# Deeper buffers for gathered rows of u, both mark tiles in one, and a final sum by DMA in place of a product with a constant

## The chip, the core and the metric

The kernel runs on one core of one Trainium2 chip. The metric is the time of one execution on the device, in microseconds; the median of three runs is compared.

## What is computed

Two transformer blocks in float32 over 512 tokens of width 1024. The change touches only the end of the second block, a layer of small experts (the reference calls it PEER). For each token and each of 8 heads it chooses 16 of 16384 experts; each expert is one row of `u` and one row of `v`, both 1024 wide:

```python
    e = i1 * N_KEYS + i2                       # chosen experts, 8 x 16 per token
    gate = jax.nn.softmax(best, axis=-1)
    u = u_exp[e]
    v = v_exp[e]
    act = jax.nn.gelu(jnp.einsum("thkd,td->thk", u, xb))
    return jnp.einsum("thk,thkd->td", (gate * act).astype(xb.dtype), v)
...
    x = x + gt2[:, None, :] * peer_ffn(h2, w_peer_q[l], peer_sub_keys[l], peer_u[l], peer_v[l])
    return rmsnorm_2(x, final_g)
```

## The kernel before

The expert layer is done in two ways side by side. The first `NS` = 128 tokens (four groups, `NG` = 4, of 32 tokens) go the sparse way: the rows of `u` and `v` that they chose are gathered from memory. The other `ND` = 384 tokens go the dense way: every expert is computed on TensorE for all of them and weighted by a table that is zero where an expert was not chosen. Float32 products are made from three products of high and low parts (`mm3`, lines 194 to 196; the parts come from `split`, ScalarE at line 148 and VectorE or GpSimd at line 149).

**Stage of the marks (lines 1569 to 1619, about 1446 to 1970 us).** A loop over 48 units of 8 dense tokens. For each unit `marks` (1575) builds two 128x128 marks per token: `G1` on VectorE (gate where the expert's first index agrees, line 1584) and `P2` on ScalarE (one where the second agrees, 1585 and 1586). Their product on TensorE (1604) is the token's table of weights, which ScalarE stages (1606) and stores to `Wd` (1594). `G1` has three buffers under the tag `whi`, `P2` three under the tag `P2`, which the routing's `eq` (1531) used before. In the same loop two experts per unit are made for all dense tokens (`expert_early`, 1417: load of 512 KB of `u`, 1357, split, 24 products, Gelu), and the generator `sparse_u` (1387) is stepped about three times a unit (1611).

`sparse_u` gathers rows of `u`: 128 steps, one for each of 32 choices and 4 groups. A step gathers 128 rows of 4 KB (32 tokens by four quarters of the choices) on GpSimd's queue (1375), and, `nb - 1` steps later, VectorE multiplies the buffer with the tokens and adds up along each row (1405). It has `nb` = 3 buffers: two halves of a tile under `wraw` and `gu3`. Both the gather and the product are kept behind what was written before them for the same engine (`keep_in_program_order`); other instructions are ordered by a planner ahead of time. The weights of the last 128 tokens come out of `pick` (1478, lines 1488 to 1493); the memory of the routing is freed after the last `pick`, and three more buffers for raw `u` (1352) lie in it.

**Stage of v (lines 1622 to 1778, about 1970 to 2550 us).** 32 blocks of four experts: `prepare` (1642) loads `v`, the table and the activations, multiplies and splits them; `products` (1672) adds into eight accumulators `O`, which take all eight PSUM banks. `sparse_v` (1678) is stepped along (1758): gathers of `v` rows into six buffers, each added with its weight into `fin` (`sacc`, 128 x 4 x 1024) by VectorE (1695, 1697). A token's sum then lies in four quarters, on four partitions 32 apart. At its end `sparse_v` brings them together with a product with a constant 0/1 matrix, `fold` (1701 to 1712), adds the residual and normalizes (1713 to 1718), and stores the first 128 tokens (1719). `bank()` there waits for a PSUM bank, and the first is free when `add(0, O[0])` has emptied it in the last block (1766 to 1777). After the last column come a sum over partitions (1782), the norm and the store of the dense tokens (1786 to 1796).

Of the kernel before, what the change touches and what calls it, by code (L numbers as in the profile page):

```python
# [10 lines left out]
F32 = mybir.dt.float32  # L11
# [3 lines left out]
AF = mybir.ActivationFunctionType  # L15
# [6 lines left out]
D = 1024  # L22
# [47 lines left out]
def tile_body(ctx: ExitStack, tc: tile.TileContext, A, out, taps=None, upto=None):  # L70
# [72 lines left out]
    def bank():  # L143
        return psum.tile([128, 512], F32, name="bank", tag="bank")
# [1242 lines left out]
    def sparse_u():  # L1387

        w2 = [wpool.tile([128, 2, D], F32, name=f"gu{i}", tag="wraw", bufs=2) for i in range(2)]
        free = [w[:, i] for w in w2 for i in range(2)]  # L1390
        hr = [xsp.tile([128, D], F32, name="hr", tag="xs") for g in range(min(NG, XS))] + free[:max(0, NG - XS)]
        bufs = free[max(0, NG - XS):] + [up.tile([128, D], F32, name="gu3")]
        nb = len(bufs)
        for g in range(NG):
            nc.sync.dma_start(hr[g], ap(Hd, 32 * g * D, [[0, 4], [D, 32], [1, D]]))
        steps = [(s, g) for s in range(32) for g in range(NG)]
        for k in range(len(steps) + nb - 1):
            if k < len(steps):
                s, g = steps[k]
                gather(bufs[k % nb], A["u_rows"], g, s)  # L1400
            if k >= nb - 1:
                s, g = steps[k - nb + 1]
                b = bufs[(k + 1) % nb]
                d = sr[:, 2, g, s:s + 1]
                tc.keep_in_program_order(nc.vector.tensor_tensor_reduce(  # L1405
                    out=b, in0=b, in1=hr[g], op0=OP.mult, op1=OP.add, scale=1.0, scalar=0.0, accum_out=d))
            yield
        nc.scalar.activation(sr[:, 3], sr[:, 2], AF.Gelu_apprx_tanh)
        nc.vector.tensor_tensor(sr[:, 3], sr[:, 3], sr[:, 1], op=OP.mult)
        while True:  # L1410
            yield
# [25 lines left out]
    with ExitStack() as ph:  # L1437
# [137 lines left out]
        def marks(n):  # L1575

            t, tok0 = divmod(NS + 8 * n, 128)
            i1, i2, gp = picks[t]
            G1 = wpool.tile([128, 8, 128], F32, name="G1", tag="whi", bufs=3)
            P2 = up.tile([128, 8, 128], F32, name="P2", bufs=3)  # L1580
            for k in range(0, 8, 4):
                for i in range(4):
                    tok = slice(tok0 + k + i, tok0 + k + i + 1)
                    nc.vector.tensor_scalar(G1[:, k + i], IOTA, i1[:, tok], gp[:, tok], op0=OP.is_equal, op1=OP.mult)
                    nc.scalar.activation(P2[:, k + i], IOTA, AF.Square, scale=-1.0, bias=i2[:, tok])
                nc.scalar.activation(P2[:, k:k + 4], P2[:, k:k + 4], AF.Relu, scale=-1.0, bias=1.0)
            return G1, P2

# [8 lines left out]
        for n in range(units):  # L1597
# [10 lines left out]
                stores.extend((n // 4, stage, e) for e in range(0, 128, 32))  # L1608
            if stores:
                store()  # L1610
            while 32 * NG + 6 > fed[0] and fed[0] * (units - 4) < (n + 1) * (32 * NG + 6):
                next(sparse)
                fed[0] += 1
            while (n + 1) * (N_EARLY * BT - routed) // units > early[0] - routed:
# [7 lines left out]
    with ExitStack() as ph:  # L1622
# [55 lines left out]
        def sparse_v():  # L1678
# [7 lines left out]
            for k in range(len(steps) + nb - 1):  # L1686
# [10 lines left out]
                        tc.keep_in_program_order(nc.vector.scalar_tensor_tensor(  # L1697
                            fin[:, g], b, w, fin[:, g], op0=OP.mult, op1=OP.add))
                yield
            x, row, sq = (b[:NS] for b in bufs[:3])  # L1700
            FOLD = bufs[4][:, :NG * NS]
            nc.sync.dma_start(FOLD, A["fold"])
            ssq = small.tile([128, 1], F32, name="fsq", bufs=1)
            nc.sync.dma_start(x, Xd[0:NS, :])
            nc.sync.dma_start(row, ap(Mv, 5 * D, [[0, NS], [1, D]]))
            for f in range(2):
                c = slice(f * 512, (f + 1) * 512)
                o = bank()
                for g in range(NG):
                    nc.tensor.matmul(o[:NS], FOLD[:, g * NS:(g + 1) * NS], fin[:, g, c], start=g == 0, stop=g == NG - 1)  # L1710
                nc.vector.tensor_tensor(row[:, c], o[:NS], row[:, c], op=OP.mult)
                nc.vector.tensor_tensor(x[:, c], x[:, c], row[:, c], op=OP.add)
            yield
            nc.vector.memset(ssq, 1.0)
            nc.scalar.activation(sq, x, AF.Square, accum_out=ssq[:NS])
            nc.sync.dma_start(row, ap(A["final_g"], 0, [[0, NS], [1, D]]))
            r = inv_rms(ssq, D, newton=True)
            nc.vector.scalar_tensor_tensor(x, x, r[:NS], row, op0=OP.mult, op1=OP.mult)
            nc.sync.dma_start(out[0:NS, :], x)
            yield  # L1720

# [27 lines left out]
        for n, b in enumerate(order[:-1]):  # L1749
            nxt = prepare(order[n + 1])  # L1750
            next(nxt, None)
            for group in (range(4), range(4, 8)):
                for i in range(0, BT, 2):
                    products(b, group, i, i + 2)
                    if group[0] or i:
                        next(nxt, None)
                k = 2 * n - 1 + (group[0] > 0)
                while n >= 1 and vfed[0] * 57 < k * (32 * NG + 5):
                    next(gathered, None)
                    vfed[0] += 1  # L1760
            for _ in nxt:
# [66 lines left out]
def lay_out(i):  # L1828
# [1 line left out]
    cols = lambda v: np.ascontiguousarray(v.reshape(-1, 128).T)  # L1830
    a = {}
    a["cst"], a["t5"] = constants()
    a["fold"] = (np.arange(128)[:, None] % 32 + 32 * (np.arange(NG * NS) // NS) == np.arange(NG * NS) % NS).astype(np.float32)
    a["x"] = i["x"][0]
    a["xT"] = a["x"].reshape(4, 128, 8, 128).transpose(0, 3, 2, 1)
    a["mem"] = i["mem"][0]
# [73 lines left out]
```

## Time and profile before

| | |
|---|---|
| median of three runs | 2561.01 us (2559.43 to 2565.94) |
| the profiled execution | 2564.41 us, of which the span is 2562.4 us |
| mean granted TensorE clock | 0.979 of 2.4 GHz |
| TensorE busy | 2452.3 us (96%) |
| VectorE busy | 1753.2 us (68%) |
| ScalarE busy | 1159.9 us (45%) |
| GpSimd busy | 509.8 us (20%) |
| DMA | 545.79 MB, mean 213 GB/s |

The span runs from the first to the last instruction; the profiled execution's own time is 2.0 us longer. Products on TensorE overlap their neighbours, so that a busy TensorE is not one at its peak: the number of products in a stretch says more. PE is TensorE, PEld its loading of weights, DVE VectorE, ACT ScalarE, POOL GpSimd, SP SyncE, whose queue issues most of the DMAs. Where a line is that of a helper (148, 149, 194 to 196, 1375), the name of the tile tells which step it is.

### The profile page before, as it was taken

Reading aid. Unit: us, or ns where it says so; the run is one execution under the profiler, and the core shown is the slowest. Engines: PE = TensorE matmul, PEld = TensorE weight load, DVE = VectorE, ACT = ScalarE, POOL = GpSimd, SP = SyncE. Lnnn points to the kernel's source line nnn. Section 1 sums busy time; section 2 is a strip of 40 time slices with the busy share of each in tenths; the row PEclk is TensorE's granted clock in tenths of the full one; section 3 lists DMA queues with packets and bytes.
Section 4 is the critical chain, followed back from the end, with each engine's and each line's share of the span. In section 5 each row is a group of like instructions: output and inputs, shape, how many; then the busy total and the mean of one; then the engine's idle time right before and its main releaser. Section 6 shows DMA issues by size and latency. Waiting matters only on the chain.

```text
span 2562.4 us, 36881 instructions
## 1 busy us (share of the span) xinstructions
PE 2452.3 (96%) x13565; PEld 2241.0 (87%) x13565; DVE 1753.2 (68%) x4163; ACT 1159.9 (45%) x2339; POOL 509.8 (20%) x389
## 2 busy tenths in 40 slices
PE   8899989999999999999997889999999999999998
PEld 7789878888878888888896789999999899999997
DVE  6467687643374567446889777777773588888884
ACT  7346464323244445224232467767675333333333
POOL 0021000000000000000043344434420144445430
PEclk9899999999999999999998889999999999999999
DMA  8511347742332221334133589999996999999981
GB/s 299 183 63 34 112 154 274 256 171 91 107 131 104 94 87 65 111 132 160 62 101 101 169 323 345 351 345 335 338 332 232 332 340 365 366 370 359 367 302 58
DMA packets 181905, 545.79 MB, mean 213 GB/s; under 512 B 17259, under 2 KB 68003, under 8 KB 170972
## 3 DMA queue, kind: packets, MB, share of 16 engines
q1 hardware_dynamic: 130592, 353.52, 40.0%
q0 software_dynamic: 38944, 139.49, 14.6%
q10 hardware_dynamic: 12188, 50.44, 5.0%
q8 instruction: 106, 1.74, 0.3%
q14 instruction: 75, 0.61, 0.1%
HBM read 480.25 MB, written 67.33 MB: 214 GB/s over the span
## 4 chain that ended last, share of the span: by engine, by line
PE 71%; DVE 10%; issue 9%; POOL 5%; DMA 3%; ACT 2%; POOLq 0%; SPq 0%; DVEq 0%; ACTq 0%
PE bank L196 21%; PE bank L194 21%; PE bank L195 20%; POOL gu L1375 5%; DVE eq L1534 1%; PE bank L1604 1%; DMA gu<-in_u_rows,eS 1%; PE bank L732 1%; PE bank L324 1%; PE bank L735 1%; DVE best L1544 1%; PE bank L323 1%; DMA adaw<-in_w_adaT 1%; PE bank L1164 1%; DVE eq L1538 1%
## 5 line engine op out<-in xcount | busy, mean ns | idle before, releaser
L194 PE MATMUL bank<-hTh,uhl 128*128 128x384 f32 x1024 | 357.7, 349 | 33.8 <-ACT uhl L148 33.8
L196 PE MATMUL bank<-hTh,uhl 128*128 128x384 f32 x1024 | 355.0, 347 | 23.9 <-DVE uhl L149 12.3
L195 PE MATMUL bank<-hTl,uhl 128*128 128x384 f32 x1024 | 352.1, 344 | 0.0
L196 PE MATMUL bank<-wah,vlo 128*128 128x384 f32 x1024 | 347.2, 339 | 0.0
L194 PE MATMUL bank<-wah,vhi 128*128 128x384 f32 x1024 | 346.0, 338 | 0.0
L195 PE MATMUL bank<-wal,vhi 128*128 128x384 f32 x1024 | 344.7, 337 | 0.0
L194 PE MATMUL bank<-hTh,whi 128*128 128x512 f32 (+1 forms) x832 | 318.4, 385 | 1.2 <-ACT hTh L148 1.2
L195 PE MATMUL bank<-hTl,whi 128*128 128x512 f32 (+1 forms) x832 | 315.4, 380 | 1.7 <-DVE hTl L149 1.7
L196 PE MATMUL bank<-hTh,wlo 128*128 128x512 f32 (+1 forms) x832 | 314.9, 379 | 0.2 <-DVE wlo L177 0.2
L1375 POOL DMA_INDIRECT gv<-in_v,eS x107 | 172.3, 1610 | 346.4 <-DVE sacc L1697 182.4
L194 PEld LDWEIGHTS bank<-hTh,uhl 128*128 128x128 f32 x1024 | 198.5, 194 | 36.0 <-ACT uhl L148 36.0
L1375 POOL DMA_INDIRECT gu<-in_u_rows,eS x128 | 178.6, 1395 | 255.1 <-DVE sr L1405 244.4
L196 PEld LDWEIGHTS bank<-hTh,uhl 128*128 128x128 f32 x1024 | 197.9, 193 | 30.9 <-DVE uhl L149 16.2
L148 ACT ACTIVATE wah<-ga 128x384 fp32r<-128x384 f32 x128 | 66.1, 518 | 349.7 <-PE bank L196 343.3
L195 PEld LDWEIGHTS bank<-hTl,uhl 128*128 128x128 f32 x1024 | 198.3, 194 | 0.0
L149 DVE TENSOR_TENSOR wlo<-wraw,whi 128x512 fp32r<-128x512 f32 (+1 forms) x200 | 129.5, 685 | 93.4 <-ACT whi L148 93.1
L196 PEld LDWEIGHTS bank<-wah,vlo 128*128 128x128 f32 x1024 | 192.4, 188 | 0.5 <-issue 0.5
L194 PEld LDWEIGHTS bank<-wah,vhi 128*128 128x128 f32 x1024 | 192.3, 188 | 0.2 <-issue 0.2
L195 PEld LDWEIGHTS bank<-wal,vhi 128*128 128x128 f32 x1024 | 192.1, 188 | 0.2 <-issue 0.2
L195 PEld LDWEIGHTS bank<-hTl,whi 128*128 128x128 f32 x832 | 158.9, 191 | 32.4 <-DVE hTl L149 2.6
L196 PEld LDWEIGHTS bank<-hTh,wlo 128*128 128x128 f32 x832 | 158.4, 190 | 32.4 <-DVE wlo L177 0.6
L194 PEld LDWEIGHTS bank<-hTh,whi 128*128 128x128 f32 x832 | 157.8, 191 | 32.0 <-ACT hTh L148 2.2
(508 smaller groups left out, 5221.0 us busy)
## 6 DMA issues: line engine op xcount, KB each, us to landing
uraw<-in_u SPq DMA_DIRECT2D x128, 512.0 KB, 6.6
vraw<-in_v SPq DMA_DIRECT2D x64, 1024.0 KB, 6.3
adaw<-in_w_adaT SPq DMA_DIRECT2D x48, 512.0 KB, 4.1
Wd<-stage ACTq DMA_DIRECT2D x48, 512.0 KB, 6.5
Wt<-Wd SPq DMA_DIRECT2D x32, 768.0 KB
GAd<-ga ACTq DMA_DIRECT2D x31, 768.0 KB
ga<-GAd SPq DMA_DIRECT2D x31, 768.0 KB, 9.6
wraw<-in_ffn_gu SPq DMA_DIRECT2D x22, 1024.0 KB, 6.6
```

Of the source, the lines that this page charges most:

```text
L148: nc.scalar.activation(hi, src, AF.Copy)
L149: (eng or nc.vector).tensor_tensor(lo, src, hi.bitcast(F32), op=OP.subtract)
L194: nc.tensor.matmul(o, l[0], r[0], start=start, stop=False)
L195: nc.tensor.matmul(o, l[0], r[1], start=False, stop=False)
L196: nc.tensor.matmul(o, l[1], r[0], start=False, stop=stop)
L323: nc.tensor.matmul(o, Q, K[:, g], start=True, stop=False)
L324: nc.tensor.matmul(o, Q, K[:, 2 + g], start=False, stop=stop)
L732: nc.tensor.matmul(o, slot[:, 0, ts(i)], v(i, 0), start=i == 0, stop=i == j)
L735: nc.tensor.matmul(o, slot[:, 1, ts(i)], v(max(0, j - 2) + i, 1), start=i == 0, stop=i == nb - 1)
L1164: nc.tensor.matmul(O[:, 128 * j + 64 * g:128 * j + 64 * g + n], pt[:, ts(i)], va[:, i, 128 * c + 64 * g:128 * c + 64 * g + n], start=i == ...
L1375: tc.keep_in_program_order(nc.gpsimd.indirect_dma_start(out=dst, out_offset=None, in_=src, in_offset=bass.IndirectOffsetOnAxis(ap=eS[:, g, ...
L1534: nc.vector.scalar_tensor_tensor(eq[:, a % 8], cf, float(offs[a]), step[:, :, a:a + 1].to_broadcast([128, 8, 16]), op0=OP.is_ge, op1=OP.mult)
```

## The change

Three things change, and two paces with them. `sparse_u` gets three more buffers, `gu4`, under the tag `P2`, which makes six; the product of a step is written five steps after its gather and no longer two. `G1` and `P2` become two halves of one tile under the tag `whi`, with three buffers, so that the tag `P2` is free for the gathers. The loop of units steps `sparse_u` so that its end still falls inside (137 steps over 45 units in place of 134 over 44).

At the end of `sparse_v` the product with `fold` goes, with its load and the constant. In its place 16 DMAs bring quarter `q` of each group `g` from partitions 32q to 32q+31 of `fin` to the partitions of the group's tokens, in `parts[q]`; three sums on VectorE add up the four parts, and the rest follows on 128x1024 tiles. The pace of `sparse_v` goes from 133 to 139 steps in 57 half blocks.

```diff
         bufs = free[max(0, NG - XS):] + [up.tile([128, D], F32, name="gu3")]
+        bufs += [up.tile([128, D], F32, name="gu4", tag="P2", bufs=3) for _ in range(3)]
         nb = len(bufs)
...
-                b = bufs[(k + 1) % nb]
+                b = bufs[(k - nb + 1) % nb]
...
-            G1 = wpool.tile([128, 8, 128], F32, name="G1", tag="whi", bufs=3)
-            P2 = up.tile([128, 8, 128], F32, name="P2", bufs=3)
+            both = wpool.tile([128, 2, 8, 128], F32, name="marks", tag="whi", bufs=3)
+            G1, P2 = both[:, 0], both[:, 1]
...
-            while 32 * NG + 6 > fed[0] and fed[0] * (units - 4) < (n + 1) * (32 * NG + 6):
+            while 32 * NG + 9 > fed[0] and fed[0] * (units - 3) < (n + 1) * (32 * NG + 9):
...
-            x, row, sq = (b[:NS] for b in bufs[:3])
-            FOLD = bufs[4][:, :NG * NS]
-            nc.sync.dma_start(FOLD, A["fold"])
+            parts, (x, row) = bufs[:4], bufs[4:6]
             ssq = small.tile([128, 1], F32, name="fsq", bufs=1)
             nc.sync.dma_start(x, Xd[0:NS, :])
             nc.sync.dma_start(row, ap(Mv, 5 * D, [[0, NS], [1, D]]))
-            for f in range(2):
-                c = slice(f * 512, (f + 1) * 512)
-                o = bank()
+            for q in range(4):
                 for g in range(NG):
-                    nc.tensor.matmul(o[:NS], FOLD[:, g * NS:(g + 1) * NS], fin[:, g, c], start=g == 0, stop=g == NG - 1)
-                nc.vector.tensor_tensor(row[:, c], o[:NS], row[:, c], op=OP.mult)
-                nc.vector.tensor_tensor(x[:, c], x[:, c], row[:, c], op=OP.add)
+                    nc.sync.dma_start(parts[q][32 * g:32 * g + 32], fin[32 * q:32 * q + 32, g])
+                yield
+                if q % 2:
+                    nc.vector.tensor_tensor(parts[q], parts[q], parts[q - 1], op=OP.add)
+            sq = parts[1]
+            nc.vector.tensor_tensor(sq, sq, parts[3], op=OP.add)
+            nc.vector.tensor_tensor(sq, sq, row, op=OP.mult)
+            nc.vector.tensor_tensor(x, x, sq, op=OP.add)
             yield
...
-                while n >= 1 and vfed[0] * 57 < k * (32 * NG + 5):
+                while n >= 1 and vfed[0] * 57 < k * (32 * NG + 11):
...
-    a["fold"] = (np.arange(128)[:, None] % 32 + 32 * (np.arange(NG * NS) // NS) == np.arange(NG * NS) % NS).astype(np.float32)
```

## Rows read from the trace of the kernel before

**Rows 1.** Stretches of the span, the columns named in the first line

```profile
core 0: us, PE busy (x) PEld busy (x) DVE busy (x) ACT busy (x) POOL busy (x), PEclk, DMA share, GB/s
1460.00:1500.00 40.00, 28.50 (x166) 27.77 (x165) 25.31 (x51) 18.66 (x42) 17.74 (x14) 0.83 0.84 301
1500.00:1910.00 410.00, 405.46 (x2521) 402.50 (x2520) 310.87 (x633) 290.21 (x628) 160.84 (x115) 1.00 0.93 339
...
2050.00:2480.00 430.00, 430.00 (x2454) 430.00 (x2453) 365.22 (x427) 147.07 (x207) 202.07 (x119) 1.00 0.99 358
```

**Rows 2.** Stretches inside the stage of marks: one without holes, one with

```profile
1530.00:1600.00 70.00, 70.00 (x441) 70.00 (x440) 54.45 (x112) 50.21 (x111) 28.62 (x20) 1.00 0.96 347
...
1730.00:1740.00 10.00, 8.42 (x45) 8.42 (x46) 9.45 (x20) 6.00 (x14) 5.23 (x4) 0.83 0.77 259
```

**Rows 3.** All waits in 1500 to 1910: total us, times, longest

```profile
POOL gu L1375 <- DVE sr L1405: 225.5, 88, 4.6
...
DVE gu L1405 <- DMA gu<-in_u_rows,eS: 97.7, 56, 4.5
...
PE bank L196 <- DVE uhl L149: 4.5, 5, 2.0
```

**Rows 4.** DMA issues in 1500 to 1910, median us to landing

```profile
uraw<-in_u SPq DMA_DIRECT2D x79, 512.0 KB, 6.9
...
gu<-in_u_rows,eS POOLq DMA_INDIRECT x115, 8.0
```

**Rows 5.** VectorE's timeline ahead of the hole at 1730: start, duration, [idle <-releaser]

```profile
1725.09 1.23 DVE L1405 CUSTOM_DVE_ANT_0 gu<-gu,hr 128x1024 f32<-128x1024 f32 x1 [1.66 <-DMA gu<-in_u_rows,eS]
...
1729.15 1.23 DVE L1405 CUSTOM_DVE_ANT_0 gu<-gu,hr 128x1024 f32<-128x1024 f32 x1 [2.83 <-DMA gu<-in_u_rows,eS]
...
1730.31 1.22 DVE L149 TENSOR_TENSOR uhl<-uraw,uhl 128x1024 fp32r<-128x1024 f32 x1
```

**Rows 6.** VectorE by line and form, 2050 to 2525: busy, mean ns, idle before

```profile
L1697 DVE SCALAR_TENSOR_TENSOR sacc<-gv,sr,sacc 128x1024 f32<-128x1024 f32 x104 | 130.4, 1277 | 0.0
```

**Rows 7.** VectorE's timeline at the start of the stage

```profile
1470.20 1.23 DVE L1405 CUSTOM_DVE_ANT_0 gu<-gu,hr 128x1024 f32<-128x1024 f32 x1 [9.16 <-DMA gu<-in_u_rows,eS]
...
1471.73 1.23 DVE L1405 CUSTOM_DVE_ANT_0 gu<-gu,hr 128x1024 f32<-128x1024 f32 x1 [0.30 <-DMA gu<-in_u_rows,eS]
...
1472.89 0.28 DVE L1488 CAST eI<-bank 128x128 int32<-128x128 f32 x1
1473.10 1.21 DVE L1405 CUSTOM_DVE_ANT_0 gu<-gu,gu 128x1024 f32<-128x1024 f32 x1
...
1475.41 0.26 DVE L1493 CAST i<-e 128x128 f32<-128x128 int32 x1
```

**Rows 8.** Waits of SP's queue, 1440 to 1500

```profile
SPq L1357 <- DVE i L1493: 14.3, 1, 14.3
```

**Rows 9.** GpSimd's timeline at the start of the stage

```profile
1462.29 0.98 POOL L1375 DMA_INDIRECT gu<-in_u_rows,eS  x1 [0.30 <-issue]
...
1471.71 0.94 POOL L1375 DMA_INDIRECT gu<-in_u_rows,eS  x1 [7.20 <-DVE sr L1405]
```

**Rows 10.** The chain of work that ended last, 2500 to 2563

```profile
2528.25 3.53 PE bank L1710 x8
...
2532.65 3.62 PE bank L1710 x8
```

**Rows 11.** SP's timeline at the end

```profile
2497.78 0.34 SPq L1704 DMA_DIRECT2D gv<-Xd  x1
```

**Rows 12.** VectorE's timeline towards the end

```profile
2496.47 2.47 DVE L1697 SCALAR_TENSOR_TENSOR sacc<-gv,sr,sacc 128x1024 f32<-128x1024 f32 x2
2503.51 0.56 DVE L149 TENSOR_TENSOR wal<-ga,wah 128x384 fp32r<-128x384 f32 x1 [4.56 <-PE bank L195]
...
2531.82 0.69 DVE L1711 TENSOR_TENSOR gv<-bank,gv 128x512 f32<-128x512 f32 x1 [3.79 <-PE bank L1710]
```

**Rows 13.** The marks' lines on ScalarE: ns min/median/max

```profile
L1585 ACT ACTIVATE P<-cst,i x384: 384/390/414, 1434.0 to 1944.9; 128x128 f32<-128x128 f32 x192
```

More of the change, by code (lines that the diff above doesn't have):

```diff
@@ L1705, in sparse_v @@
             nc.sync.dma_start(row, ap(Mv, 5 * D, [[0, NS], [1, D]]))
-            for f in range(2):
-                c = slice(f * 512, (f + 1) * 512)
-                o = bank()
+            for q in range(4):
                 for g in range(NG):
-                    nc.tensor.matmul(o[:NS], FOLD[:, g * NS:(g + 1) * NS], fin[:, g, c], start=g == 0, stop=g == NG - 1)
-                nc.vector.tensor_tensor(row[:, c], o[:NS], row[:, c], op=OP.mult)
-                nc.vector.tensor_tensor(x[:, c], x[:, c], row[:, c], op=OP.add)
+                    nc.sync.dma_start(parts[q][32 * g:32 * g + 32], fin[32 * q:32 * q + 32, g])
[6 more added lines that the diff above has]
+            nc.vector.tensor_tensor(x, x, sq, op=OP.add)
             yield
-            nc.vector.memset(ssq, 1.0)
-            nc.scalar.activation(sq, x, AF.Square, accum_out=ssq[:NS])
+            nc.scalar.activation(sq, x, AF.Square, accum_out=ssq)
             nc.sync.dma_start(row, ap(A["final_g"], 0, [[0, NS], [1, D]]))
             r = inv_rms(ssq, D, newton=True)
-            nc.vector.scalar_tensor_tensor(x, x, r[:NS], row, op0=OP.mult, op1=OP.mult)
+            nc.vector.scalar_tensor_tensor(x, x, r, row, op0=OP.mult, op1=OP.mult)
             nc.sync.dma_start(out[0:NS, :], x)
```

## Prediction

> **What bounds the kernel now.** I read the time by stage first, then the waits inside the stage that holds the gathers, then the chain of waits at the end. In the stage of the marks and the gathers of u, TensorE shows 405 of 410 us busy [rows 1]. A busy share says little here, because neighbouring products overlap, so I count products. An undisturbed stretch makes 441 in 70 us, 6.30 per us [rows 2]; the whole stage made 2521 in 410 us, which at that rate needs 400 us. So about 10 us of it are lost in single holes, the largest of which is a stretch with 45 products where 63 fit, at a clock of 0.83 [rows 2]. (The counts take in products that cross an edge, so this is good to a microsecond or two; adding up the holes alone gives some 8 us.)
>
> What makes the holes: in this stage TensorE waits only for VectorE's low parts of u (line 149), 4.5 us in 5 waits; VectorE waits 97.7 us in 56 waits for gathered rows to land; GpSimd waits 225.5 us in 88 waits for VectorE to have used a buffer [rows 3]. That is a loop: GpSimd may start gather k only when the product of gather k-3 is done, a gather needs 8.0 us to land [rows 4], and VectorE, which works in order, then stands at the next product with the low parts of u queued behind it. In the largest hole one sees it: two products with 1.66 and 2.83 us of idle time ahead of them, and the low part only after both [rows 5]. A unit of 8 tokens has 48 + 16 products in the rows, so 64 / 6.30 = 10.2 us, and carries three gathers: a buffer has one unit in which to be issued, to land and to be used. Some 9.5 us (0.3 to the issue [rows 9], 8.0, 1.2 for the product [rows 5]) stand against 10.2 us. It is on the edge, and small lateness goes through to TensorE.
>
> **Six buffers.** Gather k now waits for product k-6, so there are two units, 20 us, for the same 9.5 us. The two copies of the buffer index are equal for 3 and for 6 buffers (k+1 and k-2, k+1 and k-5 leave the same rest), so that line changes nothing. The pace stays: 137/45 steps a unit against 134/44. The last product comes some three steps, one unit, later, into a stretch where VectorE has time. The nearest row for six buffers is the stage of v: there each gather has six buffers, the DMA engines are busier (0.99 against 0.93) [rows 1], and the sums that use the rows show no idle time ahead of them in 104 instructions [rows 6]. So VectorE's 97.7 us go. What is late next is TensorE itself, for VectorE is busy 311 of 410 us and ScalarE 290 [rows 1]. Bounds: nothing gained, if the holes have another cause that shows only then, to 10 us gained, the whole loss. I take 8 us, the sum of the holes. On the other side, the raw u loads have six buffers and land in 6.9 us [rows 4], and one expert costs TensorE some 5 us (two in a unit), so they could land two or three times as late without harm.
>
> More gathers under way compete for the same DMA engines. The rows show these at 0.93 and 339 GB/s in this stage and at 0.99 and 358 GB/s in the stage of v [rows 1], so 2% more speed in this stage is there to be had, though not 6%. The Trainium skill speaks against the change here (DMA: Bandwidth & Descriptors, Queues, rings and completion order): a DMA engine goes round its queue rows and takes a whole packet from each that has work, so a gather queue that always has work takes its turn each time and the raw loads of u land later. No run here shows that yet; if it went so far that TensorE waited for raw u, the 8 us would drop out of the sum, which is rival (2).
>
> **The start of this stage.** Here 166 products were made in 40 us [rows 1], where 252 would fit: 13.6 us lost, part of it at a lower granted clock (0.83 over the stretch). It is a different chain. VectorE stands at the first product until gather 0 lands at 1470.2, does a second one, and only then the casts of the last pick, 1472.89 to 1475.41 [rows 7]. The next raw loads stand on SP's queue for that last cast, 14.3 us [rows 8], because their new buffers lie in the memory that the routing frees. The change moves the first product one unit later in the program's text, but product 0 is still pinned only behind marks that were made long before, and it needs the same gather, started at the same time. I therefore leave both first products ahead of the casts. The third product (at 1473.10, between the casts) goes behind the next marks, which gives about 1.2 us; three more gathers start at once (gather 3 had waited till 1471.71 [rows 9]), and 3 x 0.52 MB at 358 GB/s is up to 4.4 us of DMA work ahead of the raw loads. Bounds: 13.6 us gained, if the casts come first, to 4.4 us lost; I take 0.
>
> **Both marks in one tile.** No instruction is added or removed. The tile has as many buffers as each had (three), so the distance from unit to unit stays. Cost nothing, if the two halves are tracked apart (below).
>
> **Quarters by DMA, no constant.** The products with the constant are 16 instruction records at the very end. They need a PSUM bank, all eight are taken by the accumulators, so they run when the first accumulator is emptied, in the middle of the last block. There they lie on the chain that ended last with 3.53 and 3.62 us [rows 10], 7.15 us; products follow without a hole to the end. With them gone the chain of the last columns is the same, 7.15 us earlier. The sums now need no PSUM, so they can run one block earlier. Added: 16 DMAs of 128 KB, at 0.34 us of SP each [rows 11] 5.4 us of issuing; three sums, a product and a sum of 128x1024 on VectorE, 5 x 1.22 = 6.1 us by the low part of the same size [rows 5], against four halves of 0.69 us [rows 12], 2.8 us, before. No row shows such a DMA between partitions. The nearest are the loads of 512 KB, 6.9 us [rows 4]; I take 7 us for a quarter. Its cover: the last accumulation ends at 2498.9 [rows 12]; the pace in the stage of v rises by 139/133, so that it ends two half blocks earlier, and a block of 96 products at 175 ns (below) is 16.8 us; VectorE idles 4.56 us at 2503, waiting for TensorE to free buffers [rows 12]. So 6.1 us of sums are hidden. Queued behind the 16 DMAs on SP are the last loads of v, a block ahead of their use. If a sum is put ahead of the last low parts, VectorE stands for a quarter twice, up to 2 x (4 x 0.34 + 7) = 17 us, of which at least 4.6 are covered: a cost between 0 and 12 us. I take 0, since by then VectorE has no accumulations left (133/57 = 2.3 in a half block, 3 us). The faster pace adds under 1% to the traffic of a stage that runs at TensorE's own rate (2454 products in 430 us [rows 1], 175 ns each): nothing.
>
> **The sum.** 8 + 7.15 = 15 us. Against its own time (2564.41, span 2562.4) the profiled execution would come to about 2549; the median of the runs is 3.4 us lower, 2561.0, and from it I forecast 2546.
>
> **Rivals.** (1) The casts come before the first products: then the start's stall goes too. For it: the first products stand a unit later in the text. Against: only what is ready decides there, and that has not moved. 2546 - 13 = 2533. (2) Only the constant's products are saved, because the holes in the u stage stay: with six gathers always under way the raw loads of u land later than TensorE needs them, and the waits change their name. For it: DMA engines at 0.93. Against it: the lead of the raw loads, and [rows 6]. 2561 - 7 = 2554. (3) VectorE stands for quarters ahead of the last splits. 2546 + up to 12 = 2558; for it, that landing takes longer than an order made beforehand allows for. (4) Slower: the marks in one tile are tracked as one, so VectorE's and ScalarE's halves, written in turns, wait for each other. A unit would then hold VectorE for 8 x 0.39 us of ScalarE's marks [rows 13], 3.1 us, on top of the 7.7 us it is busy (311/410 of 10.2): 10.8 against 10.2, 0.6 us in each of 48 units, about 30 us; with the end's 7 us off, 2584. It decides against us as soon as a unit grows by 0.32 us (15/48). Against it: two gathers go into the halves of one tile, and product 0 read one half at 1470.2 while the other landed for 1471.73 [rows 7]; no wait there for the tile as a whole. (5) The change doesn't bite: the gathers are still paced by something else and the sums still land at the very end; 2561.
>
> **How the numbers follow.** Forecast 0.55, (1) 0.15, (2) 0.13, (3) 0.08, (4) and a start that gets worse together 0.06, (5) 0.03. The range, 2532 to 2556, holds the forecast with its bounds, (1), (2) and a part of (3). About 0.3%, 7.7 us, can be told from no change. Faster by more: the forecast nearly always, (1), and a little of (2) and (3), 0.75. Within it: most of (2) and (3), and (5), 0.18. Slower: (4) and a bad start, 0.07.
>
> **What would show it.** Right: VectorE waits for gathers of u only at the start, GpSimd still waits for products, and the stage from 1500 on holds 6.3 products per us throughout; the last block's products run without a break of 7 us, and the store of the first 128 tokens leaves before the last block. Wrong: TensorE waits for raw u; VectorE shows waits for quarters between the last low parts; VectorE's marks wait for ScalarE's; the hole at 1473 is gone or longer.

## The result and the profile after

The changed kernel takes 2545.57 us (median of five runs, 2539.86 to 2551.52), against 2561.01 before (five runs beside it, 2559.43 to 2572.09). The ratio of the two, run side by side, is 0.993, with a 95% interval of 0.9913 to 0.9946, so 14 to 22 us less. The forecast was 2546. The profiled execution took 2545.55 us, with a span of 2543.8 us and a mean granted clock of 0.977.

Where the span's 18.6 us went can be read from four instants of the two traces. Two of them are the first and the last product of the marks. The rows below give them as first and last start of a group of products, with the routing scores ahead of them (name of the tile, then ns of the shortest, the median and the longest, then first and last start); before:

```profile
L1466 PE MATMUL bank<-skT,pq x128: 270/275/422, 1208.1 to 1293.4; 128*128 128x128 f32 x128
L1604 PE MATMUL bank<-G,P x768: 270/275/276, 1460.8 to 1964.6; 128*128 128x128 f32 x192
```

and after (line numbers are one higher in this part of the file):

```profile
L1467 PE MATMUL bank<-skT,pq x128: 270/275/582, 1206.4 to 1291.7; 128*128 128x128 f32 x128
L1605 PE MATMUL bank<-marks x768: 270/275/275, 1463.0 to 1954.5; 128*128 128x128 f32 x192
```

The first and the last of the eight additions that empty the accumulators, before and after (start, duration, [idle <-releaser] on VectorE):

```profile
2527.41 0.62 DVE L1738 SCALAR_TENSOR_TENSOR acc<-bank,modc,acc 128x384 f32<-128x384 f32 x1 [2.26 <-PE bank L196]
2549.30 0.62 DVE L1738 SCALAR_TENSOR_TENSOR acc<-bank,modc,acc 128x384 f32<-128x384 f32 x1 [1.49 <-PE bank L196]
```

```profile
2515.86 0.62 DVE L1739 SCALAR_TENSOR_TENSOR acc<-bank,modc,acc 128x384 f32<-128x384 f32 x1 [2.24 <-PE bank L196]
2530.62 0.62 DVE L1739 SCALAR_TENSOR_TENSOR acc<-bank,modc,acc 128x384 f32<-128x384 f32 x1 [1.49 <-PE bank L196]
```

| stretch | before, us | after, us | difference |
|---|---|---|---|
| start to the first product of the marks | 1460.8 | 1463.0 | +2.2 |
| first to last product of the marks | 503.8 | 491.5 | -12.3 |
| to the first addition of the last block | 562.8 | 561.4 | -1.4 |
| first to last addition | 21.9 | 14.8 | -7.1 |
| last addition to the end of the span | 13.1 | 13.2 | +0.1 |

The second and the fourth line hold the two terms of the forecast. Of the second line's 12.3 us, 8.3 come from the steady part of the stage, counted below; some 3 come from 1460 to 1500, where after made 186 products and before 166, and that stretch differs between executions of one kernel (170 in a repeat of the changed kernel). The first line is not the change's: the profiled execution of before was quick in the routing, 167.4 us from the last score to the first mark, while after shows 171.3 us and a kernel with the routing and the marks exactly as before shows 171.0 (the one with the quarters alone, below).

**The stage of the marks and the gathers of u.** The stretches of [rows 1] and [rows 2], in the changed kernel (us, then PE, PEld, DVE, ACT, POOL busy with their counts, PEclk, DMA share, GB/s):

```profile
1460.00:1500.00 40.00, 32.79 (x186) 32.06 (x186) 24.79 (x54) 18.64 (x43) 17.14 (x14) 0.86 0.88 319
1500.00:1910.00 410.00, 410.00 (x2573) 410.00 (x2572) 313.77 (x640) 297.74 (x645) 175.21 (x114) 1.00 0.96 350
...
1730.00:1740.00 10.00, 10.00 (x64) 10.00 (x63) 7.83 (x16) 8.00 (x18) 4.10 (x3) 1.00 0.94 318
2050.00:2480.00 430.00, 430.00 (x2454) 430.00 (x2453) 363.21 (x426) 145.44 (x206) 190.12 (x117) 1.00 0.99 360
```

The stage makes 2573 products where [rows 1] had 2521; 52 products at 6.30 per us are 8.3 us. The ten microseconds from 1730 hold 64 products at full clock, where [rows 2] had 45 at 0.83. DMA rises from 0.93 to 0.96, as the same bytes move in less time. All waits over 20 us in 1500 to 1910 (total, times, longest):

```profile
POOL gu L1375 <- DVE sr L1406: 185.9, 39, 6.0
ACT ga L1366 <- PE bank L196: 98.4, 78, 2.3
DVE uhl L149 <- ACT uhl L148: 47.3, 22, 2.8
DVE marks L1585 <- PE bank L1605: 26.7, 10, 2.7
POOL gu L1375 <- issue: 22.9, 75, 0.3
```

VectorE's 97.7 us for gathered rows and TensorE's 4.5 us for low parts [rows 3] have no row any more. In their place VectorE's marks wait for TensorE to have used a buffer: VectorE is now ahead, and TensorE waits for nothing in this stage. GpSimd still waits for products, which costs nothing: its 114 instructions in this stretch are all gathers, so nothing that TensorE lacks stands behind one.

**The start.** VectorE's timeline at the place of [rows 7], and SyncE's wait of [rows 8]:

```profile
1468.74 1.23 DVE L1406 CUSTOM_DVE_ANT_0 gu<-gu,hr 128x1024 f32<-128x1024 f32 x1 [8.14 <-issue]
...
1471.44 1.23 DVE L1406 CUSTOM_DVE_ANT_0 gu<-gu,hr 128x1024 f32<-128x1024 f32 x1 [1.47 <-DMA gu<-in_u_rows,eS]
...
1472.59 0.29 DVE L1489 CAST eI<-bank 128x128 int32<-128x128 f32 x1
...
1473.97 0.23 DVE L1494 CAST i<-e 128x128 f32<-128x128 int32 x1
1474.11 2.14 DVE L1585 TENSOR_SCALAR marks<-cst,i,gp 128x128 f32<-128x128 f32 x8
1476.17 1.21 DVE L1406 CUSTOM_DVE_ANT_0 gu<-gu,gu 128x1024 f32<-128x1024 f32 x1
```

```profile
SPq L1357 <- DVE i L1494: 13.2, 1, 13.2
```

The two first products still stand ahead of the casts, and only the third has gone behind the next marks. From the first cast to the last are 1.38 us, where [rows 7] have 2.52, so the third product's 1.2 us have left that stretch. The next raw loads wait 13.2 in place of 14.3 us.

**The end.** SyncE's queue and VectorE, 2450 to 2510:

```profile
2465.50 10.04 SPq L1707 DMA_DIRECT2D gv<-sacc  x11
2475.58 1.86 SPq L1707 DMA_DIRECT2D gu<-sacc  x3
```

```profile
2468.13 1.27 DVE L1698 SCALAR_TENSOR_TENSOR sacc<-gv,sr,sacc 128x1024 f32<-128x1024 f32 x1
2482.19 1.22 DVE L1710 TENSOR_TENSOR gv<-gv 128x1024 f32<-128x1024 f32 x1
...
2496.31 1.22 DVE L1714 TENSOR_TENSOR gv<-gv,gv 128x1024 f32<-128x1024 f32 x1
```

The last of the five operations of the sums (1714, the sum with the residual) ends at 2497.5, a block ahead of the first addition at 2515.86; VectorE shows no wait for a quarter. The two pieces of 3.53 and 3.62 us in [rows 10] are gone, and the eight additions come every 2.11 us without a break.

### The profile page after: what moved, and what is told of

It reads as the page before. It is cut to its first block, busy times and chain, and to the rows that moved or that the text cites. A ratio compares the mean times of both kernels' runs of the same rounds, so it can differ in the third digit from the quotient of the medians.

```text
span 2543.8 us, 36880 instructions
## 1 busy us (share of the span) xinstructions
PE 2443.9 (96%) x13549; PEld 2240.7 (88%) x13549; DVE 1753.4 (69%) x4163; ACT 1160.1 (46%) x2339; POOL 518.3 (20%) x389
## 5 line engine op out<-in xcount | busy, mean ns | idle before, releaser
L196 PE MATMUL bank<-hTh,uhl 128*128 128x384 f32 x1024 | 353.7, 345 | 15.9 <-POOL uhl L149 10.2
L1375 POOL DMA_INDIRECT gu<-in_u_rows,eS x128 | 192.7, 1505 | 229.3 <-DVE sr L1406 201.7
L149 DVE TENSOR_TENSOR uhl<-uraw,uhl 128x1024 fp32r<-128x1024 f32 x99 | 122.9, 1242 | 107.5 <-ACT uhl L148 82.8
```

The costliest lines, as they stand in the source:

```text
L149: (eng or nc.vector).tensor_tensor(lo, src, hi.bitcast(F32), op=OP.subtract)
L196: nc.tensor.matmul(o, l[1], r[0], start=False, stop=stop)
L1375: tc.keep_in_program_order(nc.gpsimd.indirect_dma_start(out=dst, out_offset=None, in_=src, in_offset=bass.IndirectOffsetOnAxis(ap=eS[:, g, ...
```

## The experiments

All ratios are to the kernel before, run on the same chip in turns. My theory: the gain is the holes that the loop of three buffers left in the stage of the marks (about 8 us), plus the 7.15 us of products with the constant that stood in the last block, and the two are independent. Rivals: the gain is one of the two alone; the marks' common tile costs or gains; the first stall of the stage (13.6 us) is worth its length.

### The parts one by one

**Six buffers alone.** The kernel before, with the six buffers, the one tile for both marks (without it the tag of the new buffers isn't free) and the pace of the gathers of u; the product with the constant stays.

```diff
+        bufs += [up.tile([128, D], F32, name="gu4", tag="P2", bufs=3) for _ in range(3)]
...
-            G1 = wpool.tile([128, 8, 128], F32, name="G1", tag="whi", bufs=3)
-            P2 = up.tile([128, 8, 128], F32, name="P2", bufs=3)
+            both = wpool.tile([128, 2, 8, 128], F32, name="marks", tag="whi", bufs=3)
+            G1, P2 = both[:, 0], both[:, 1]
...
-            while 32 * NG + 6 > fed[0] and fed[0] * (units - 4) < (n + 1) * (32 * NG + 6):
+            while 32 * NG + 9 > fed[0] and fed[0] * (units - 3) < (n + 1) * (32 * NG + 9):
```

> The kernel before with six buffers for the gathers of u, both marks in one tile and the pace of 137/45, but with the product with the constant at the end as before. My theory (the loop of gather, landing and product sets the holes): the stage from 1500 to 1900 us shows no wait of VectorE for gathers and 6.3 products per us throughout; the time is 8 to 10 us below the kernel before, ratio about 0.9965, and the two L1710-like groups at the end still take 7.15 us. Rival (the gain of the whole change came from the end and from the order of the work around it): ratio 0.998 to 1.0.

Measured: 2553.29 against 2565.26 us, ratio 0.9954 (0.9939 to 0.9969). The stage from 1500 to 1890, the only row of a wait for gathered rows' buffers in it, and the chain at the end:

```profile
1500.00:1890.00 390.00, 390.00 (x2447) 390.00 (x2446) 302.05 (x615) 281.82 (x611) 171.27 (x114) 1.00 0.97 351
```

```profile
POOL gu L1375 <- DVE sr L1406: 187.8, 39, 6.0
```

```profile
2517.00 3.53 PE bank L1711 x8
2521.41 3.62 PE bank L1711 x8
```

The holes are gone with the buffers alone, and the 7.15 us at the end are still there. The median gain of 12 us is larger than the 8 to 10 us that I had expected; the interval, 8 to 16 us, holds both.

**Quarters alone.** The changed kernel with the u stage of before (three buffers, two tiles for the marks, the old pace); the end of v as changed:

```diff
-            FOLD = bufs[4][:, :NG * NS]
-            nc.sync.dma_start(FOLD, A["fold"])
+            parts, (x, row) = bufs[:4], bufs[4:6]
...
-                    nc.tensor.matmul(o[:NS], FOLD[:, g * NS:(g + 1) * NS], fin[:, g, c], start=g == 0, stop=g == NG - 1)
+                    nc.sync.dma_start(parts[q][32 * g:32 * g + 32], fin[32 * q:32 * q + 32, g])
...
-                while n >= 1 and vfed[0] * 57 < k * (32 * NG + 5):
+                while n >= 1 and vfed[0] * 57 < k * (32 * NG + 11):
```

> The kernel before with three buffers and two separate marks, but with the quarters brought together by DMA, without the product with the constant, at the pace of 139 steps. My theory: the last block's products run without a break, 7.15 us less, ratio about 0.997; the waits of VectorE for gathers of u stay at about 98 us and the holes with them. Rival (the sums by DMA hold VectorE and SP up, and the whole gain came from the gathers): ratio 0.9995 to 1.002.

Measured: 2559.17 against 2565.26 us, ratio 0.9977 (0.9964 to 0.9989). The additions of the last block run without a break, from 2530.01 to 2544.78, 14.8 us as in the changed kernel, while the waits of the u stage (1500 to 1890) stay as in [rows 3]:

```profile
DVE gu L1405 <- DMA gu<-in_u_rows,eS: 91.2, 56, 4.8
...
PE bank L196 <- DVE uhl L149: 3.9, 6, 1.5
```

**The marks' common tile alone.** Three buffers, the old end.

```diff
-            G1 = wpool.tile([128, 8, 128], F32, name="G1", tag="whi", bufs=3)
-            P2 = up.tile([128, 8, 128], F32, name="P2", bufs=3)
+            both = wpool.tile([128, 2, 8, 128], F32, name="marks", tag="whi", bufs=3)
+            G1, P2 = both[:, 0], both[:, 1]
```

> The kernel before with both marks in one tile and nothing else; the three buffers under the tag P2 stay empty in the stage of the marks. My theory: nothing changes, ratio 1.000 within 0.002; waits of VectorE for gathers as before, about 98 us. Rival (marks in one tile tie VectorE and ScalarE to each other): 0.6 us more in each of 48 units, about 30 us, ratio 1.012.

Measured: 2561.99 against 2565.26 us, ratio 0.9995 (0.9981 to 1.001). The waits in 1500 to 1890 are those of before:

```profile
DVE gu L1405 <- DMA gu<-in_u_rows,eS: 91.0, 51, 4.2
```

So the tile is free, the buffers are worth 12 us (8 to 16) and the quarters 6 us (3 to 9). The product of the three ratios, 0.9954 x 0.9977 x 0.9995 = 0.9926, agrees with 0.993 for the whole: the parts add up.

### How many buffers

**Two buffers** in the kernel before:

```diff
-        bufs = free[max(0, NG - XS):] + [up.tile([128, D], F32, name="gu3")]
+        bufs = free[max(0, NG - XS):]
```

> The kernel before with two buffers for the gathers of u in place of three. My theory (a loop of issue 0.3, landing 8.0 and product 1.2 us for each buffer): three gathers a unit with two buffers need 3 x 9.5 / 2 = 14.3 us where a unit has 10.2, so the 43 units of gathers take 43 x 14.3 = 610 us in place of about 445: about 150 us slower, 2710 us, less where gathers land sooner on emptier DMA engines (at 6.5 us: 12 us a unit, 75 us slower). Rival (the holes come from VectorE's order alone, whatever the number of buffers): under 10 us slower.

Measured: 2670.24 against 2564.12 us, ratio 1.0412 (1.0372 to 1.0451). The stage from 1500 to 1890 and its waits:

```profile
1500.00:1890.00 390.00, 324.10 (x1870) 316.43 (x1869) 236.16 (x472) 216.06 (x469) 128.65 (x91) 0.92 0.78 270
```

```profile
DVE gu L1405 <- DMA gu<-in_u_rows,eS: 151.4, 65, 5.7
...
PE bank L196 <- DVE uhl L149: 65.9, 24, 7.3
```

This is the chain of the holes at large: DMA stands idle more (0.78), rows come late, VectorE stands at the products, the low parts behind them come late, TensorE waits 65.9 us and its granted clock sinks to 0.92. The 128 gathers run from 1460.7 to 2006.9, so one each 546.2 / 127 = 4.30 us, and the loop of two buffers takes 8.6 us.

**Four buffers** in the changed kernel:

```diff
-        bufs += [up.tile([128, D], F32, name="gu4", tag="P2", bufs=3) for _ in range(3)]
+        bufs += [up.tile([128, D], F32, name="gu4", tag="P2", bufs=3) for _ in range(1)]
```

> The changed kernel with one more buffer for rows of u in place of three (four buffers; paces, marks' tile and quarters as changed). My theory: the loop of a buffer (issue 0.3, landing 8, product 1.2, some 9.5 us) has to fit into (buffers / 3) units of 10.2 us. Two buffers give 6.8 us, three 10.2, four 13.6, so four are already clear of the edge by 4 us and the stage of the marks should run without holes as with six: some 64 to 65 products in each 10 us, no wait of TensorE in 1500 to 1890, VectorE's waits for gathered rows under 10 us (three buffers: 91 to 98), time within 2 us of the changed kernel, ratio about 0.993. Rival: landings scatter far around their median, so that four buffers take away only a part of the holes; then VectorE still waits 30 us or more for rows, and the ratio lies near 0.995 to 0.996.

Measured: 2551.99 against 2567.79 us, ratio 0.9937 (0.9922 to 0.9952). In 1500 to 1890:

```profile
1500.00:1890.00 390.00, 390.00 (x2448) 390.00 (x2447) 303.19 (x615) 279.93 (x604) 168.50 (x116) 1.00 0.96 348
```

```profile
DVE gu L1406 <- DMA gu<-in_u_rows,eS: 15.8, 15, 2.0
```

As many products as with six (2448), though VectorE still waits 15.8 us for rows, more than the 10 us that I had set. Those waits fit into its idle time. One buffer more is enough for the holes from 1500 us on. It may not be enough for the start. The kernel with six buffers that ran beside it (with the sums late, below) took 2540.34 to 2549.29 us, below every run of this one (2549.42 to 2557.18). With four buffers two products of gathered rows stand between the casts of the last pick (one with three buffers, none with six). The next raw loads wait 17.5 us for the last cast, 12.3 with six buffers, and 1460 to 1500 holds 126 products in place of 182. These are single traces, the one with four buffers of its slowest run, and no run has the number of buffers as the only difference from the kernel beside it; so what the last two buffers are worth stays open, up to some 6 us by the medians.

### Where the sums of the quarters fall

The changed kernel with the old pace in the stage of v, so that the quarters and sums are written behind the fourth column of the last block:

```diff
-                while n >= 1 and vfed[0] * 57 < k * (32 * NG + 11):
+                while n >= 1 and vfed[0] * 57 < k * (32 * NG + 5):
```

> The changed kernel with the pace in the stage of v put back to 133 steps in 57 half blocks, so that the quarters and their sums are the last six steps and are written behind the fourth column of the last block. It tells what the cover of the sums is worth. My theory: the gain of the DMA form comes from its freedom from PSUM; the sums need only VectorE and SyncE, both of which have time in the last block, but VectorE works in order, so up to two stands for a quarter and 6 us of sums come between the additions of the last columns. TensorE waits for none of this before the last column. I expect 0 to 4 us more than the changed kernel (ratio 0.993 to 0.995). Rival (the third of the prediction, VectorE standing for quarters ahead of work that TensorE needs): 8 to 17 us more, so that the whole gain of the end is gone (ratio 0.996 or more). Second rival: the order made beforehand goes by readiness and not by the place in the text, so nothing moves at all: within 1 us, with the quarters at 2455 to 2477 us as in the changed kernel.

Measured: 2545.89 against 2567.79 us, ratio 0.9909 (0.9891 to 0.9926). SyncE's queue, then VectorE:

```profile
2486.24 10.42 SPq L1707 DMA_DIRECT2D gv<-sacc  x12
2496.75 3.35 SPq L1707 DMA_DIRECT2D gu<-sacc  x4
```

```profile
2517.03 1.22 DVE L1710 TENSOR_TENSOR gu<-gu,gv 128x1024 f32<-128x1024 f32 x1
2518.28 1.23 DVE L1712 TENSOR_TENSOR gv<-gv,gu 128x1024 f32<-128x1024 f32 x1
2519.43 0.61 DVE L1739 SCALAR_TENSOR_TENSOR acc<-bank,modc,acc 128x384 f32<-128x384 f32 x1
2519.95 1.21 DVE L1713 TENSOR_TENSOR gv<-gv,gv 128x1024 f32<-128x1024 f32 x1
...
2534.14 0.62 DVE L1739 SCALAR_TENSOR_TENSOR acc<-bank,modc,acc 128x384 f32<-128x384 f32 x1 [1.49 <-PE bank L196]
```

The quarters went out some 20 us later and the sums fell among the additions, yet nothing was lost; I had expected 0 to 4 us (ratio 0.993 to 0.995), and the ratio lies below that. Three of the eight additions come 0.9 to 1.4 us late against the changed kernel's step of 2.11 us, and VectorE has caught up by the last; TensorE, whose next columns go into other banks, shows no wait for them. From the last product of the marks (1956.6 here, 1958.8 in the repeat of the changed kernel, below) to the last addition are 577.5 us, against 2536.39 - 1958.8 = 577.6 in the repeat and 576.1 in the changed kernel's first trace. So the gain of the end comes from the products that are gone and not from the place of the sums: VectorE standing for quarters, the third rival, has no price here in either place.

### The first stall of the stage

**The casts first.** The last `pick` is written ahead of the four last early experts, so that its casts come before the first products:

```diff
+        pick(NT - 1, *found.pop())
         for _ in range(E_LAST):
             expert_early(nc.gpsimd)
-        pick(NT - 1, *found.pop())
```

> The changed kernel with the last pick written ahead of the last four experts of the routing, so that its four casts stand on VectorE ahead of the first products of gathered rows. My theory (the stall at the start is the casts' wait for gather 0 to land, which holds the next raw loads back): the hole of about 10 us at 1473 goes, and the time is 8 to 13 us below the changed kernel, ratio to the kernel before about 0.989. Rival (the raw loads of u land late there since six gathers are ahead of them on the DMA engines): the hole stays within 3 us of its length, ratio as the changed kernel, 0.993.

Measured: 2544.62 against 2565.26 us, ratio 0.9929 (0.9915 to 0.9944). The stretch of the stall, and TensorE's waits from 1435 to 1500:

```profile
1460.00:1500.00 40.00, 40.00 (x254) 40.00 (x253) 27.97 (x54) 25.68 (x55) 23.25 (x18) 1.00 0.93 337
```

```profile
PE bank L1482 <- DVE ei L1554: 10.0, 1, 10.0
```

The hole is gone: 254 products, as an undisturbed stretch has. But the ratio is that of the changed kernel. TensorE's transposes of the last pick (1482) now stand ahead of the experts in its queue and wait 10.0 us for the end of VectorE's routing; the experts that had covered this are behind them. The stall has moved ahead by more than 30 us: TensorE's longest wait ends at 1448.1 here and at 1482.0 in the changed kernel.

**Between the experts.** The same `pick` behind the first, the second or the third of the four experts (`m` = 0, 1, 2), of which the last two ran beside a repeat of the changed kernel:

```diff
-        for _ in range(E_LAST):
+        for i in range(E_LAST):
             expert_early(nc.gpsimd)
-        pick(NT - 1, *found.pop())
+            if i == m:
+                pick(NT - 1, *found.pop())
```

> The changed kernel itself, beside the kernels of this job on the same chip. Expected: ratio to the kernel before about 0.993, the hole of 13 us at the start of the stage as in its first trace, and no wait of VectorE for gathers from 1500 us on.

> The changed kernel with the last pick (its casts free the memory for the next raw u) written behind the first of the four last early experts, one earlier than in the version that gave 0.990 and one later than ahead of all four, which gave 0.993. My theory: the place of the pick trades two stands of TensorE against each other, one for the high parts of u behind the casts' own input (10 us when the pick is first) and one for raw loads that wait for the last cast (13.6 us when it is last); between them lies a place where both are covered by the experts already loaded. Behind the first expert I expect one wait of some 4 to 7 us at 1440 to 1460 and none at 1460 to 1500, 226 to 254 products in 1460 to 1500, ratio 0.990 to 0.992. Rival: the version behind the second expert was faster by chance of its order, and all places give 0.991 to 0.993.

> As the kernel with the pick behind the third expert, but behind the second. In its order one product of gathered rows stands ahead of the first low part of u on VectorE. My theory: the routing's result comes just as TensorE is done with two experts, so at most 2 us of waiting; the low part behind the first product is late by the landing of gather 0, some 8 us, of which one expert of work is covered: between the changed kernel and the kernel with three, ratio 0.990 to 0.993.

> The changed kernel with the last pick written behind the third of the four last experts of the routing, so that the casts still stand ahead of the first products of gathered rows but TensorE has three experts to do until the routing's result is there. My theory (moved in front of all four experts, the pick cost TensorE 10 us of waiting for the routing, about what the hole at 1473 had cost; with work ahead of it neither is lost): no wait of TensorE over 3 us from 1440 to 1500 us, and 8 to 12 us below the changed kernel, ratio to the kernel before about 0.989. Rival (the 13 us are lost in any order, since the last raw loads of the routing and six gathers meet on the DMA engines): within 3 us of the changed kernel.

| last pick behind | median, us | ratio (95%) | TensorE's waits 1435 to 1500, us |
|---|---|---|---|
| no expert | 2544.62 | 0.9929 (0.9915 to 0.9944) | 10.0 |
| the first | 2541.70 | 0.9897 (0.9878 to 0.9915) | 5.9 |
| the second | 2538.14 | 0.9900 (0.9874 to 0.9926) | 3.9 + 2.5 + 0.9 |
| the third | 2541.07 | 0.9910 (0.9888 to 0.9933) | 3.1 + 2.2 + 1.8 |
| all four (changed kernel, repeated) | 2547.48 | 0.9930 (0.9910 to 0.9950) | 9.1 + 1.8 + 0.3 |

TensorE's waits behind the second expert:

```profile
PE bank L1482 <- DVE ei L1554: 3.9, 1, 3.9
PE bank L196 <- DVE uhl L149: 2.5, 1, 2.5
PE bank L196 <- POOL uhl L149: 0.9, 1, 0.9
```

The kernel before took 2565.26 us beside the first line, 2567.79 beside the second and 2564.12 beside the other three, so across these groups only the ratios can be compared. Each place trades the wait for the routing (1482) against waits for parts of u: from 1460 to 1500 the five lines hold 254, 245, 226, 194 and 170 products. Part of what is left comes from the gathers: behind the second expert, TensorE's 2.5 us end at 1467.9, when it gets a low part that VectorE made from 1466.6, behind a product that had stood 8.15 us for gather 0. The three places between have ratios of 0.990 to 0.991, and behind the second expert all four runs (2535.92 to 2540.58) lie below all six of the changed kernel beside it (2544.34 to 2551.32), though the intervals of the two ratios overlap. Which of the three places is best isn't told by these intervals. My expectations missed in part: behind the third expert I had set 8 to 12 us of gain, behind the second at most 2 us of waiting for the routing (3.9 measured) and a time above that of the third. Of the 13.6 us that [rows 1] shows as lost at the start, the places behind the third and the second expert win back 6.4 and 9.3 us by the medians against the repeat.

## Why the prediction was right

**The holes.** Forecast 8 us. From 1500 to 1890 us the three traces with three buffers hold 2396, 2407 and 2412 products, the one with four 2448 and those with six 2447 to 2450: the holes cost 6 to 8 us of this stretch, and the forecast was worked out on the trace with the most. The buffers alone brought 8 to 16 us by the ratio, so the forecast lies at the lower edge of that. Why the middle of this is 12 and not 8 is open: the stretch from 1460 to 1500 held 166 products before, 186 after, 196 with six buffers alone, but also 173 and 185 in the two other kernels with three buffers, 170 in the repeat of the changed kernel, and 126 with four, so it differs between executions (and by the instant at which the stage starts) by more than the rest. The mechanism is shown by the row of buffer numbers: two give 65.9 us of TensorE waiting in 390 us, three 4.5, four and six none. My loop of 9.5 us against one unit of 10.2 was right in kind, and with four buffers, where the loop has 13.6 us, the steady part has no hole. With two buffers it was somewhat too long: 8.6 us were measured, where DMA was less busy, and the loss was 106 us where the loop of 9.5 us would give 150.

**The rows of the v stage as nearest rows** [rows 6] told rightly that six buffers leave VectorE no wait. The second rival was that six gathers under way make the raw loads of u too late for TensorE. No wait of any engine for raw u has a row in 1500 to 1910, before or after, so if they came later here, it was inside their lead, and the rival falls. The Trainium skill (DMA: Bandwidth & Descriptors, Queues, rings and completion order) says that a DMA engine goes round the queue rows that have work, a packet from each; how much later the raw loads land by this, no run here shows.

**The start.** Forecast: the order of the products and casts stays, the third product goes behind the next marks for 1.2 us, taken as 0. The trace shows just that: the third product is gone from between the casts, and these take 1.1 us less from the first to the last. The first rival (the casts first, 2533) did not come about, and its price of 13 us was too high. I gave it the stall's whole length, because I had looked only at what ends the wait. In the four kernels that have the casts ahead of the first products, the `pick` is also moved on TensorE; the one with it ahead of all four experts gained nothing by its ratio, and the two that ran beside a repeat gained 6.4 and 9.3 us. The casts alone, without TensorE's part of the `pick`, were not moved in any run.

**The marks' tile.** Forecast 0, measured 0.9995 (0.9981 to 1.001). The fourth rival, 30 us for halves that wait for each other, falls.

**The products with the constant.** Forecast 7.15 us from two pieces of the chain; the last block's additions took 7.1 us less.

**The quarters.** The term that was mis-sized: I took 0.34 us of SyncE for each from a plain load [rows 11], 5.4 us for 16; the trace shows

```profile
L1707 SPq DMA_DIRECT2D gv<-sacc x12: 507/588/1727, 2455.4 to 2474.9; - x12
```

(ns, least, median and most), so 16 take over 9 us at the median. 14 of them stand in the queue from 2465.5 to 2477.4, 12 us with one wait of 2.1 us for VectorE's last accumulation among them, and the next load of activations and two loads of `v` come behind them. It cost nothing, because those loads are issued a block ahead of their use: TensorE has no wait in 2440 to 2530, and the only wait of that stretch for a load is VectorE's 0.5 us for one tile of activations, at 2455, ahead of these 14. The 7 us that I took for a quarter to land have no row; no engine waits for a quarter, not even with the sums late.

**The sum.** 15 us were forecast; the medians shown give 15.4, the ratio 14 to 22. The two terms are each inside the interval of their own experiment, the 8 us only just. That the median came within half a microsecond of 2546 is luck: five runs of the changed kernel spread over 12 us, and the middle of the ratio's interval stands for 18 us.

## What to carry to other kernels

Price a ring of buffers by its loop (issue, landing, use) against what one turn of the consumer takes: here 9.5 us stood against 10.2, TensorE showed only 4.5 us of waits while VectorE beside it showed 97.7, and the holes were worth 8 us. One buffer more took them away; whether a deeper ring brings more has to be looked for where the ring starts, too. An operation that needs a PSUM bank can only run when a bank is free, whenever its data were ready; here it stood at the end of a kernel that fills all banks, and moving its data by DMA took its whole length, 7.1 us, off the chain. A stall that is cured by moving a step ahead has to be priced with what the step is moved past, on every engine's queue: here the 13 us hole became a 10 us hole earlier, and only a place between won part of it.

## What the runs showed of the hardware that was not expected

A DMA of 128 KB from 32 partitions to 32 others holds SyncE's queue for 0.59 us (median), against 0.34 us for a plain load of 512 KB [rows 11]: the smaller transfer takes the queue longer.

VectorE's small casts and integer operations of the last two picks take 0.23 to 0.29 us each in most places. But with the `pick` behind the second expert, and also behind the third, the last two of ten took 2.3 to 2.4 us, and behind the first expert the last but one did. VectorE, then GpSimd, behind the second:

```profile
1452.32 0.23 DVE L1492 CAST i<-e 128x128 f32<-128x128 int32 x1
1452.58 2.38 DVE L1493 TENSOR_SCALAR e<-eI 128x128 int32<-128x128 int32 x1
1455.00 2.31 DVE L1494 CAST i<-e 128x128 f32<-128x128 int32 x1
```

```profile
1452.49 4.74 POOL L149 TENSOR_TENSOR uhl<-uraw,uhl 128x1024 fp32r<-128x1024 f32 x2 [13.16 <-ACT uhl L148]
```

GpSimd makes two low parts of about 2.4 us each; the first ends at 1454.88 and the first long operation at 1454.96, the second ends at 1457.23 and the second long one at 1457.31. Behind the first expert GpSimd works from 1461.01 to 1463.41 and then stands until 1464.29:

```profile
1461.10 2.39 DVE L1493 TENSOR_SCALAR e<-eI 128x128 int32<-128x128 int32 x1
1463.53 0.23 DVE L1494 CAST i<-e 128x128 f32<-128x128 int32 x1
```

The first of these ends with GpSimd's instruction, and the last cast, which falls where GpSimd stands, takes 0.23 us again. The kernel before shows it on a mark (1584): one that starts at 1443.57 takes 2.15 us in place of 0.34 and ends at 1445.72, just behind a GpSimd instruction that ran from 1443.25 to 1445.64. So these small operations, where they start just behind a GpSimd low part, end with it. The Trainium skill (SBUF — State Buffer, SBUF: two separate sides) says that VectorE and GpSimd share a pair of ports, which a GpSimd instruction or a VectorE instruction of certain kinds (in a mode that uses two ports, or with two inputs in SBUF) holds for its whole length if it starts first. These rows agree for the operations shown; that it is the ports, no run here shows. The long operations are not what TensorE waits for: with the `pick` behind the third expert its 3.1 us for low parts of VectorE end at 1483.2 and 1489.8, more than 15 us later.
